# Alternating heads in the chunk products of a recurrence, with an accumulator bank for each head

## The chip, the cores and the metric

One core of a Trainium2 chip runs the whole computation as one program. The metric is the device time of the program in microseconds; the time before is the median of three runs. The engines are TensorE (PE, with its weight loads shown as PEld), VectorE (DVE), ScalarE (ACT), GpSimd (POOL) and SyncE (SP), which issues most DMAs.

## The reference, cut to what matters

Two transformer-like blocks run one after the other on a sequence of 1024 tokens of width 1024, in float32. The first has attention and a state space model side by side, then a gated feed-forward. The second has a retention mixer (4 heads of 128) and an RWKV-7 mixer (8 heads of 64) side by side, then a feed-forward and a gated embedding. The change lies in the RWKV-7 mixer, a recurrence over time with a 64 by 64 state for each head:

```
def step(state, inp):
    r_t, w_t, k_t, v_t, kk_t, b_t = inp
    sa = einsum('bhvk,bhk->bhv', state, -kk_t)
    state = state * w_t[:, :, None, :] + sa[..., None] * b_t[:, :, None, :] + v_t[..., None] * k_t[:, :, None, :]
    return state, einsum('bhvk,bhk->bhv', state, r_t)
```

The kernel computes it by chunks of 64 steps. Within a chunk, the products of all pairs of steps (s, t) of the keys (k and b = kk * a, each divided by the running decay) with the queries (-kk and r, each times the running decay) are one matrix product per head, masked to s < t or s <= t.

## The kernel before, in words

The program has stages in a row: the first block, its feed-forward, then `phase_mixers` (the retention and the recurrence of the second block, about 1365 to 1990 us of the profile), then its output projection, feed-forward and final gate. A planner orders the instructions of each engine when the program is built: an instruction's priority is its place in the order of issue, moved ahead by the number given to `high_priority`, and the planner takes, at each point of its own timeline, the ready instruction of highest priority. At run time each engine works through its order.

In `phase_mixers` generators are merged step by step, in proportion to weights; each `yield` ends a step. The recurrence has 16 quarters (4 pairs of heads by 4 quarters of the sequence; a quarter has 4 chunks of 64 for each of two heads). At step i four generators of it run beside each other: `rw_chain` of quarter i-2 (moved ahead by 300), `rw_tail` of i-3 (not moved ahead), `rw_solve` of i-1 (100) and `rw_pre` of i (200). With them run the retention (`ret_all`) and the projections (`rw_proj`), not moved ahead, whose products of three float32r matmuls each (`mm3`, line 149) are most of TensorE's work.

`rw_pre` holds the change. It builds AR (queries, two heads in partitions 0 to 63 and 64 to 127) and KB (keys, likewise; its halves are written by VectorE at line 1498 and GpSimd at line 1507, one head after the other). Then, head by head, four products of KB and AR (line 1514), one per chunk, each over 64 partitions, go into one accumulator bank of the tag "r0", and VectorE masks the bank into AA[:, h] (line 1517). The trace prints the tag as r. Parts of AA go to memory by eight small DMAs (line 1523) and come back re-ordered as As (line 1525), on which `rw_solve` begins with fifteen rounds on VectorE (line 1563). The rest of `rw_pre` transposes KB (line 1531) and prepares VU and the bonus.

The tag "r0" has two banks. `rw_pre` uses them for five further results (lines 1474, 1529, 1536, 1543), `rw_solve` for its products (line 1592, 1597 and 1604, written with the chunks in the outer loop and the heads in the inner), and `rw_tail` for its transposes (line 1692), which VectorE reads at line 1697. A product of float32 shows in the trace as two weight loads and two matmul records.

Of the kernel before, what the change touches and what calls it, by code (L numbers as in the profile page):

```python
# [13 lines left out]
ALU = mybir.AluOpType  # L14
# [52 lines left out]
class Builder:  # L67
# [1368 lines left out]
    def rw_pre(self, n, p, ps, B, D):  # L1436
# [5 lines left out]
        V, G, AC, TE = nc.vector, nc.gpsimd, nc.scalar, nc.tensor  # L1442
# [11 lines left out]
        def tmp(tag, bufs=1):  # L1454
            return self.t(p, [128, 256], tag=tag, bufs=bufs)
# [4 lines left out]
        a, s = tmp("a", 2), tmp("s", 2)  # L1460
# [23 lines left out]
        AR = D["AR"] = self.t(p, [128, 4, 2, 64], tag="AR", bufs=3)  # L1484
# [8 lines left out]
        KB = self.t(p, [128, 4, 2, 64], tag="KB", bufs=2)  # L1493
        V.scalar_tensor_tensor(d, k, kkw, a, ALU.mult, ALU.mult)
        yield
        for h in range(2):
            q = slice(64 * h, 64 * h + 64)
# [7 lines left out]
        for h in range(2):  # L1505
            q = slice(64 * h, 64 * h + 64)
            G.tensor_tensor(KB[q, :, h], ch(u)[q], ch(Pi)[q], ALU.mult)
            yield
        AA = D["AA"] = self.t(p, [128, 2, 4, 2, 64], tag="AA", bufs=3)
        for h in range(2):  # L1510
            q = slice(64 * h, 64 * h + 64)
            pa = self.t(ps, [128, 4, 2, 64], tag="r0", bufs=2)
            for c in range(4):
                TE.matmul(pa[:, c].rearrange("p m t -> p (m t)"), KB[q, c].rearrange("p m s -> p (m s)"),  # L1514
                          AR[q, c].rearrange("p m t -> p (m t)"), start=True, stop=True)
            yield
            V.tensor_tensor(AA[:, h], pa, B["mask"].unsqueeze(1).to_broadcast([128, 4, 2, 64]), ALU.mult)
            yield
        ds = self.t(self.dram, [4, 2, 4, 16, 16], tag="ds", bufs=2)
        for h in range(2):  # L1520
            for b in range(4):
                o = 64 * (1 - h) + 16 * b
                self.store("d").dma_start(ds[:, 1 - h, b].rearrange("c j i -> j c i"), AA[o : o + 16, h, :, 0, 16 * b : 16 * b + 16])
        A = D["A"] = self.t(p, [128, 256], tag="As", bufs=ASB)
# [19 lines left out]
        for c in range(4):  # L1544
            for h in range(2):
                q = slice(64 * h, 64 * h + 64)
                TE.matmul(pv[q, c], ch(v)[q, c], self.C["fold"][q], start=True, stop=True)
        yield
        for h in range(2):
            q = slice(64 * h, 64 * h + 64)  # L1550
# [3 lines left out]
    def rw_solve(self, n, p, ps, B, D):  # L1554
# [26 lines left out]
        def per(f):  # L1581
            px = self.t(ps, [128, 4, 64], tag="r0", bufs=2)
            for c in range(4):
                for h in range(2):
                    f(px[H[h], c], h, c)
            return px
# [9 lines left out]
        yield  # L1596
        px = per(lambda o, h, c: TE.matmul(o, D["AA"][H[h], 1 - h, c, 0], Mt[H[h], c], start=True, stop=True))
        yield
# [12 lines left out]
    def rw_chain(self, n, p, ps, B, D):  # L1611
# [4 lines left out]
        H = [slice(0, 64), slice(64, 128)]  # L1616
        AR, AA, KBt, TT, VU, pc = (D[x] for x in ("AR", "AA", "KBt", "TT", "VU", "pc"))
        if qt == 0:
            self.rwS = None
        py = self.t(ps, [128, 4, 64], tag="ry", bufs=1)  # L1620
        for c in range(4):
            S = self.rwS
            px = self.t(ps, [128, 64], tag="rc", bufs=1)
            for h in range(2):
                TE.matmul(px[H[1 - h]], AA[H[h], h, c, 0], VU[H[h], c, h], start=True, stop=S is None)
                if S is not None:
# [27 lines left out]
            for h in range(2):  # L1654
                TE.matmul(py[H[h], c], AA[:, h, c, 1], VU[:, c, h], start=True, stop=S is None)
                if S is not None:
# [570 lines left out]
```

## Time and profile before

| | |
|---|---|
| median of 3 runs | 2825.08 us (2824.87 to 2826.22) |
| the profiled execution's own time | 2825.83 us |
| its span, first to last instruction | 2824.1 us |
| TensorE busy | 2739.6 us, 97% of the span |
| VectorE busy | 1762.4 us, 62% |
| ScalarE, GpSimd busy | 1138.1 us (40%), 631.0 us (22%) |
| mean granted TensorE clock | 0.982 of full speed |

Busy time is the time in which an engine had an instruction under way; records of TensorE overlap, so a row of x16 lasts from the first start to the last end. The chain that ended last is followed back from the last instruction of the program; an engine's share of it says how much of the time that engine's work was what the end waited for. In the timeline, neighbouring instructions of one engine and one line are merged, with their count behind the x; the rows of weight loads are left out here.

### The profile page before, as it was taken

To read this page: it belongs to the slowest core of one execution; us is meant where nothing else is said; L and a number is where in the kernel's file an instruction comes from. 1 tells how busy PE (TensorE), PEld (TensorE's weight loads), DVE (VectorE), ACT (ScalarE), POOL (GpSimd) and SP (SyncE) were. 2 spreads that over 40 slices of the span, in tenths; PEclk is the share of its full clock that TensorE was granted. 3 is DMA by queue.
4 is the path that set the end of the run, shared out by engine and by line. 5 is a ranking of instruction groups with operands and counts; after the bars stand their busy time and mean duration, and the time that the engine had idled before them with its cause. 6 is when DMAs were issued, how large, how long until landed. Compare 5 with 4: busy or idle time off the path is not lost.

```text
span 2824.1 us, 44346 instructions
## 1 busy us (share of the span) xinstructions
PE 2739.6 (97%) x16624; PEld 2282.3 (81%) x16624; DVE 1762.4 (62%) x3481; ACT 1138.1 (40%) x2210; POOL 631.0 (22%) x1096
## 2 busy tenths in 40 slices
PE   7998998999999999999999999999999999999998
PEld 6987987877878888887888788887787878888887
DVE  6654667378666665463656675775558666665463
ACT  4233566444333344455333333334434333344352
POOL 5024533143111110030132231424131111110010
PEclk9999998999999999999999999999999999999999
DMA  4111020243545566565211211213714545576532
GB/s 144 47 42 55 14 86 15 90 149 101 175 161 186 178 226 211 190 208 183 63 55 41 57 54 41 57 46 103 254 53 141 173 166 180 179 278 204 171 127 86
DMA packets 173808, 352.10 MB, mean 125 GB/s; under 512 B 37785, under 2 KB 83065, under 8 KB 173593
## 3 DMA queue, kind: packets, MB, share of 16 engines
q1 hardware_dynamic: 152248, 277.43, 30.0%
q0 software_dynamic: 21344, 71.84, 7.2%
q8 instruction: 130, 2.13, 0.3%
q14 instruction: 86, 0.70, 0.1%
HBM read 246.90 MB, written 102.30 MB: 124 GB/s over the span
## 4 chain that ended last, share of the span: by engine, by line
PE 73%; issue 11%; DVE 6%; DMA 4%; POOL 3%; ACT 3%; SPq 0%; POOLq 0%; DVEq 0%; ACTq 0%
PE y L149 19%; PE mm L149 16%; PE x L149 7%; PE o L149 6%; PE z L149 6%; PE tr L149 3%; PE r L1514 1%; PE r L1604 1%; PE tr L200 1%; PE ry L1657 1%; POOL rp L641 1%; PE u L149 1%; PE o L758 1%; DVE w L104 1%; DMA td<-w_dn 1%
## 5 line engine op out<-in xcount | busy, mean ns | idle before, releaser
L103 ACT ACTIVATE w<-raw 128x1024 fp32r<-128x1024 f32 (+1 forms) x324 | 286.3, 889 | 407.5 <-PE y L149 140.2
L104 DVE TENSOR_TENSOR w<-raw,w 128x1024 fp32r<-128x1024 f32 (+1 forms) x324 | 330.4, 1024 | 121.7 <-ACT w L103 109.4
L149 PE MATMUL y<-h,w 128*128 128x512 f32 x1152 | 286.8, 390 | 4.8 <-DVE v L353 3.3
L149 PE MATMUL y<-w,h 128*128 128x512 f32 x1152 | 267.3, 391 | 0.0
L149 PE MATMUL mm<-w,h 128*128 128x256 f32 (+1 forms) x1632 | 260.3, 300 | 2.1 <-ACT w L103 2.1
L149 PEld LDWEIGHTS y<-h,w 128*128 128x128 f32 x1152 | 215.5, 188 | 51.5 <-DVE v L353 4.9
L149 PEld LDWEIGHTS y<-w,h 128*128 128x128 f32 x1152 | 215.1, 188 | 44.5 <-ACT mix L1260 0.3
L149 PEld LDWEIGHTS mm<-w,h 128*128 128x128 f32 x1632 | 221.3, 191 | 22.1 <-ACT w L103 2.9
L149 PE MATMUL y<-hx,w 128*128 128x512 f32 x960 | 233.8, 391 | 1.2 <-ACT hx L103 0.9
L149 PEld LDWEIGHTS y<-hx,w 128*128 128x128 f32 x960 | 180.5, 189 | 40.9 <-ACT hx L103 1.8
L104 DVE TENSOR_TENSOR h<-dr,h 128x512 fp32r<-128x512 f32 x154 | 102.5, 687 | 136.2 <-ACT h L103 131.1
L149 PE MATMUL mm<-h,w 128*128 128x512 f32 x672 | 183.1, 408 | 4.1 <-DVE lx L1377 2.6
L149 PE MATMUL o<-w,h 128*128 128x512 f32 x768 | 182.1, 393 | 2.8 <-DVE mix L1270 1.6
L149 PE MATMUL x<-h,w 128*128 128x512 f32 x672 | 175.3, 392 | 0.0
L149 PEld LDWEIGHTS o<-w,h 128*128 128x128 f32 x768 | 142.4, 188 | 33.3 <-DVE mix L1270 2.2
L103 ACT ACTIVATE h<-dr 128x512 fp32r<-128x512 f32 x154 | 92.8, 624 | 176.4 <-DMA dr<-ff 82.3
L149 PE MATMUL mm<-w,xh 128*128 128x256 f32 x768 | 155.2, 297 | 4.6 <-ACT qk L631 3.4
L376 DVE TENSOR_TENSOR t<-raw,raw 128x512 f32<-128x512 f32 x40 | 29.5, 738 | 189.2 <-DMA raw<-w_ffn 189.2
L149 PEld LDWEIGHTS x<-h,w 128*128 128x128 f32 x672 | 124.8, 188 | 26.2 <-ACT w L103 0.9
L149 PEld LDWEIGHTS mm<-h,w 128*128 128x128 f32 x672 | 120.1, 190 | 31.9 <-DVE lx L1377 2.8
L149 PE MATMUL z<-h,w 128*128 128x512 f32 x576 | 143.6, 396 | 1.9 <-ACT s L367 1.1
L251 POOL DMA_DIRECT2D ff<-v x66 | 36.4, 552 | 474.7 <-DVE v L361 467.1
(527 smaller groups left out, 5503.4 us busy)
## 6 DMA issues: line engine op xcount, KB each, us to landing
raw<-w_ffn SPq DMA_DIRECT2D x88, 512.0 KB
dr<-ff SPq DMA_DIRECT2D x70, 512.0 KB
ff<-v POOLq DMA_DIRECT2D x88, 256.0 KB, 3.1
td<-w_dn SPq DMA_DIRECT2D x44, 512.0 KB
td<-td POOLq DMA_DIRECT2D x44, 512.0 KB, 3.7
raw<-td SPq DMA_DIRECT2D x40, 512.0 KB
ff<-sd POOLq DMA_DIRECT2D x66, 256.0 KB, 4.9
raw<-w_dn SPq DMA_DIRECT2D x30, 512.0 KB
```

The lines of the kernel that those rows point to most:

```text
L103: self.nc.scalar.activation(hi, src, AF.Copy)
L104: self.nc.vector.tensor_tensor(lo, src, hi, ALU.subtract)
L149: return self.nc.tensor.matmul(*a, **kw, skip_group_check=more)
L200: nc.tensor.transpose(p[:, 128 * j : 128 * j + 128], xs[j][:, 128 * k : 128 * k + 128], self.ident)
L251: self.store("v").dma_start(self.part(("ff", {(0, 0): 0, (1, 0): 1, (1, 1): 2}[m, n]), f // 2), v)
L376: V.tensor_tensor(t[:, lo], r[1][:, lo], r[0][:, lo], ALU.subtract)
L641: nc.gpsimd.tensor_tensor(o, a, b, ALU.mult)
L758: nc.tensor.matmul(po, l, r, start=l is am, stop=False)
L1514: TE.matmul(pa[:, c].rearrange("p m t -> p (m t)"), KB[q, c].rearrange("p m s -> p (m s)"), AR[q, c].rearrange("p m t -> p (m t)"), start= ...
L1604: px = per(lambda o, h, c: TE.matmul(o, E[H[h], c], W[H[h], c], start=True, stop=True))
L1657: TE.matmul(py[H[h], c], AR[H[h], c, 1], S[H[h]], start=False, stop=True)
```

## The change

The two accumulators are taken first, one for each head. The eight products of a quarter are issued in one step, chunks in the outer loop and heads in the inner one. The two masked copies follow, each in a step of its own. `rw_pre` has three yields here where it had four.

```diff
         AA = D["AA"] = self.t(p, [128, 2, 4, 2, 64], tag="AA", bufs=3)
+        pa = [self.t(ps, [128, 4, 2, 64], tag="r0", bufs=2) for _ in range(2)]
+        for c in range(4):
+            for h in range(2):
+                q = slice(64 * h, 64 * h + 64)
+                TE.matmul(pa[h][:, c].rearrange("p m t -> p (m t)"), KB[q, c].rearrange("p m s -> p (m s)"),
+                          AR[q, c].rearrange("p m t -> p (m t)"), start=True, stop=True)
+        yield
         for h in range(2):
-            q = slice(64 * h, 64 * h + 64)
-            pa = self.t(ps, [128, 4, 2, 64], tag="r0", bufs=2)
-            for c in range(4):
-                TE.matmul(pa[:, c].rearrange("p m t -> p (m t)"), KB[q, c].rearrange("p m s -> p (m s)"),
-                          AR[q, c].rearrange("p m t -> p (m t)"), start=True, stop=True)
-            yield
-            V.tensor_tensor(AA[:, h], pa, B["mask"].unsqueeze(1).to_broadcast([128, 4, 2, 64]), ALU.mult)
+            V.tensor_tensor(AA[:, h], pa[h], B["mask"].unsqueeze(1).to_broadcast([128, 4, 2, 64]), ALU.mult)
             yield
```

## Rows read from the trace of the kernel before

**Rows 1.** The page: busy time of two engines, and the chain that ended last.
```profile
PE 2739.6 (97%) x16624; PEld 2282.3 (81%) x16624; DVE 1762.4 (62%) x3481; ACT 1138.1 (40%) x2210; POOL 631.0 (22%) x1096
...
PE 73%; issue 11%; DVE 6%; DMA 4%; POOL 3%; ACT 3%; SPq 0%; POOLq 0%; DVEq 0%; ACTq 0%
```

**Rows 2.** Stretches: length, busy PE, PEld, DVE, ACT, POOL, clock, DMA share, GB/s.
```profile
1365.00:1910.00 545.00, 541.26 (x5298) 455.08 (x5296) 370.83 (x1161) 196.90 (x559) 161.59 (x309) 1.00 0.18 52
```

**Rows 3.** Line 1514 (ns min/median/max); the chain by line, 1365 to 1990 us.
```profile
L1514 PE MATMUL r<-AR,KB x256: 272/272/400, 1370.1 to 1908.7; 64*128 64x128 f32 x128
...
by line: PE mm L149 48.7%; PE r L1514 4.7%; PE r L1604 4.4%; PE ry L1657 4.0%; PE ry L1655 3.5%; PE rc L1645 1.8%; issue 1.8%; PE rc L1634 1.7%; PE rc L1625 1.7%; PE r L1597 1.6%; PE r L1692 1.5%; PE r L1475 1.3%; DMA As<-ds 1.3%; PE rt L17
```

**Rows 4.** Order on TensorE, heads together (start us, us, engine, line, count).
```profile
1370.15 1.71 PE L1514 MATMUL r<-AR,KB 64*128 64x128 f32 x16
...
1907.27 1.71 PE L1514 MATMUL r<-AR,KB 64*128 64x128 f32 x16
1908.91 0.34 PE L1625 MATMUL rc<-VU,AA 64*64 64x64 f32 x4
```

**Rows 5.** Order on TensorE where the tail is near, one quarter of the middle.
```profile
1807.64 0.44 PE L1692 MATMUL r<-c_fold,yc 64*64 64x64 f32 x6
...
1809.79 1.16 PE L1514 MATMUL r<-AR,KB 64*128 64x128 f32 x8
1810.88 1.09 PE L149 MATMUL mm<-w,h 128*128 128x256 f32 x7
...
1813.79 1.16 PE L1514 MATMUL r<-AR,KB 64*128 64x128 f32 x8
1814.87 0.27 PE L1692 MATMUL r<-c_fold,yc 64*64 64x64 f32 x1
```

**Rows 6.** The same, the first and the last such quarter.
```profile
1476.41 0.32 PE L1692 MATMUL r<-c_fold,yc 64*64 64x64 f32 x2
1476.67 1.16 PE L1514 MATMUL r<-AR,KB 64*128 64x128 f32 x8
...
1480.89 1.16 PE L1514 MATMUL r<-AR,KB 64*128 64x128 f32 x8
...
1879.50 1.16 PE L1514 MATMUL r<-AR,KB 64*128 64x128 f32 x8
```

**Rows 7.** Order on TensorE, in the two split quarters without a tail.
```profile
1389.57 1.26 PE L1514 MATMUL r<-AR,KB 64*128 64x128 f32 x12
...
1393.83 0.48 PE L1514 MATMUL r<-AR,KB 64*128 64x128 f32 x2
...
1778.00 0.71 PE L1514 MATMUL r<-AR,KB 64*128 64x128 f32 x4
1778.64 0.33 PE L1634 MATMUL rc<-X,TT 64*64 64x64 f32 x4
1778.90 0.71 PE L1514 MATMUL r<-AR,KB 64*128 64x128 f32 x4
1779.54 0.62 PE L149 MATMUL mm<-w,h 128*128 128x256 f32 x3
```

**Rows 8.** Waits of TensorE, then VectorE: us in total, times, longest.
```profile
PE ry L1655 <- ACT VU L1636: 1.7, 3, 0.9
PE rc L1634 <- DVE TT L1607: 1.3, 2, 0.9
...
DVE Tm L1563 <- POOL As L1526: 21.6, 14, 3.9
```

**Rows 9.** A loop over chunks outside and heads inside, in the solve.
```profile
1445.44 0.68 PE L1592 MATMUL r<-c_ident,M 64*64 64x64 f32 x16
```

**Rows 10.** Order on VectorE: KB, masked copies, and the tail's read of its bank.
```profile
1815.59 0.48 DVE L1697 SCALAR_TENSOR_TENSOR ysq<-r,c_rwc,bv 128x256 f32<-128x256 f32 x1
...
1905.95 1.28 DVE L1498 TENSOR_TENSOR KB<-d,Pi 64x256 f32<-64x256 f32 x2
...
1908.46 1.29 DVE L1517 TENSOR_TENSOR AA<-r,c_rwmask 128x512 f32<-128x512 f32 x2
```

## The prediction

> **What bounds the kernel now.** I read the busy shares and the chain of waits first, then the stretches, then the order of instructions on TensorE around line 1514. TensorE is busy 97% of the span, and the chain that ended last lies 73% on it [rows 1]. The edited lines run only in the recurrence, and there TensorE is the bound: 541.26 of 545.00 us busy at a granted clock of 1.00 (the 2.4 GHz level), VectorE 370.83 [rows 2]. TensorE's longest waits there come to 1.7 and 1.3 us in total, before the chain's products and not before line 1514 [rows 8]. So in this stretch a microsecond taken off TensorE's queue should come off the span, less whatever wait appears behind it. The 256 records of line 1514 carry 4.7% of the chain between 1365 and 1990 us, 29 us [rows 3].
>
> **What one quarter costs now.** Each of the 16 quarters has 8 products (2 heads by 4 chunks), and each product shows as two records, so 16 a quarter. One head alone is "x8", 1.16 us from first start to last end; the next work starts 1.09 us after it (1809.79 to 1810.88) [rows 5]. One record lasts 0.272 us [rows 3], so the eight starts spread over 0.89 us, about 0.11 us apart. Three patterns occur.
> Seven quarters have both heads back to back: x16, 1.71 us, next work after 1.64 us; the first and the last are shown [rows 4]. That is less than twice 1.09, because records of the second head already run beside the last ones of the first: 16 starts fit in 1.71 - 0.27 = 1.44 us, where two heads in a row would take twice 0.89.
> Nine quarters have the heads apart, which costs twice 1.09 = 2.17 us. In seven of these (one in the middle, the first and the last are shown) the tail's products of line 1692 are around them, so the tail holds one of the two "r0" banks [rows 5, 6]. In the other two no tail is near: other products stand between the heads and inside the second one, which is x2 and x2 behind an x12 in one, and x4 and x4 in the other [rows 7].
>
> **The change part by part.** Nothing is computed that was not computed before: 8 products and 2 masked copies a quarter stay.
> *The order of the products.* Heads use different halves of the partitions. The trace has a loop of just this form, chunks outside and heads inside: line 1592 with 16 records in 0.68 us, each about 0.22 us long, so 16 starts in 0.46 us [rows 9]. The blocks of one head show records 0.11 us apart for 128 columns; with 64 columns and two heads at once, 0.46 us for 16 is two records per 0.06 us. Two streams there run side by side at full pace. So I take an alternated block as long as one head alone: 16 starts in 0.89 us, next work after 1.09 us.
> Seven quarters: 7 x (1.64 - 1.09) = 3.85 us. The two split ones without a tail: the eight products are now issued in one step of the generator, with nothing of the other generators between them: 2 x (2.17 - 1.09) = 2.2 us.
> The Trainium skill ("TensorE: Matmul & The Clock Gate", Part 3, "The mechanism") says that matmuls start and end strictly in program order. By that a head's second record would hold back the other head's first, one more step of 0.11 us per quarter, and the sum below would be 1.2 us smaller. The 0.46 us of line 1592 has no room for the extra step; the row decides.
> *Both accumulators at once.* Now the first two products need both r0 banks. In the seven quarters with a tail, the second bank is free only once line 1697 has read the tail's result. The planner puts whatever is ready first, so head 0's four products can still go alone and head 1's after that read: the old order, nothing won. Upper bound, if the tail moves out of the way each time: 7 x 1.08 = 7.6 us. Lower bound, below nothing: head 1 has started up to 2.2 us before line 1697 began, recycling the bank of head 0 (1813.79 against 1815.59 plus 0.48 [rows 5, 10], so 2.3 us to the end of the read); if TensorE simply stood for that in all seven, it loses 7 x 2.3 = 16 us. I take two of seven quarters won, 2.2 us: in six of the other quarters that have a tail it is already finished before line 1514, so small shifts of phase decide, while the nearest rows all show the bank held.
> *The masked copies.* Two on VectorE, 1.29 us in a row [rows 10]. They already come back to back behind a contiguous block; the chunk matrix then would be complete at 1907.27 + 1.16 + 1.29 = 1909.7, where it is now (1908.46 + 1.29). So nothing is won or lost for the DMA behind it. In the two splits without a tail it is complete up to 4 us sooner (the second head's records begin at 1393.83 in the one, 4.3 us behind the first's [rows 7]); the wait behind it (VectorE at line 1563 for the reloaded matrix, 21.6 us over 14 times [rows 8]) is hidden by TensorE's other work, and I count nothing.
> *One step fewer in the generator.* From four yields to three, so everything behind it in each quarter is offered slightly earlier and the planner orders the recurrence anew. Cost unknown in sign. The nearest rows are split blocks: a head cut in two takes 0.64 + 0.64 us to the next work, 0.2 us more than 1.09 [rows 7]. The small products of the chain, the solve and the tail are cut like that all over the stretch; twenty cuts more or fewer are plus or minus 4 us. I take zero and keep this for the range.
>
> **The sum.** 3.85 + 2.2 + 2.2 = 8.2 us off TensorE's queue. TensorE's idle time is under 1% there; I let 0.9 us be given back to new waits: 7.3 us. The profiled execution took 2825.83 us (span 2824.1), so 2818.5; the median of before lies 0.75 us lower, so about 2818 us.
>
> **The rivals.**
> 1. *The heads stay apart where a tail is near, and part of the rest is lost.* Only 3.85 + 2.2 = 6.0 us, or less where head 1's half of KB comes behind head 0's (the two writes of line 1498 take 1.28 us one after the other [rows 10]). With a few cuts more: 1 to 5 us off, 2822 us. For it: all seven tail rows. Against it: a later phase could free them. The Trainium skill ("TensorEngine Tiling (Array Packing)", "PSUM Bottleneck") says that tiling speeds TensorE but not the emptying of the accumulators, which can become the limit. By it the 3.85 us would not come, since the two masked copies end where they end now: 8.2 - 3.85 = 4.4 us, less what is given back, 2822 too. The trace agrees on when the copies end [rows 4, 10], but TensorE, not the copies, has no idle time [rows 2], so I hold it for the less likely.
> 2. *Every quarter alternates in full.* 3.85 + 2.2 + 7.6 = 13.6 us: 2812 us. For it: in six quarters the tail is done in time already. Against it: the tail is issued at the lowest priority, and its bank stays taken from its first product to the end of line 1697's read, 8.4 us in the quarter of the middle (1807.64 to 1816.07 [rows 5, 10]).
> 3. *The bank ring starves, slower.* Place: TensorE at head 1's first product, waiting for line 1697. With all products of a quarter in one step at high priority, the plan has them in front of work that would have filled the wait; behind the waiting product stand all the chain's and the retention's products, since TensorE issues in order. Price up to 16 us, against 6.0 us won in the other nine: 2835 us at worst, and 2832 us with 1.9 us of standing in each (13 - 6.0). It decides from 0.9 us of standing per tail quarter on (6.0 / 7). For it: the second head now always asks for the bank that the tail holds. Against it: the planner does not place a product whose bank it believes taken, so only its misjudgement counts.
>
> **How the numbers follow.** My forecast 0.33, rival 1 0.30, rival 2 0.20, rival 3 0.17. Within 0.2% (5.65 us, about what can be told from no change) lies rival 1; faster are the forecast and rival 2, 0.53; slower is rival 3, 0.17. The range from 2809 to 2831 leaves out the far ends of rivals 2 and 3. The forecast's own range is 2814 to 2820.
>
> **What would show it.** Line 1514 as x16 in about 1.16 us per quarter, and its share of the chain falling from 29 to 18 us, shows the alternation; x8 in 1.16 us next to line 1692 shows rival 1. A wait of TensorE on VectorE's line 1697, at line 1514, shows rival 3. If line 1514 falls as forecast and the stretch does not shorten, the new plan gave the time back, and the pieces of the other small products will be more. Wrong outright: 16 records that still take 1.7 us, so that heads do not run side by side at 128 columns.

## The result, and the profile after

The changed kernel takes 2846.82 us (median of 4 runs, 2843.67 to 2850.41), the kernel before 2824.97 on the same chip (4 runs, 2823.23 to 2826.22): a ratio of 1.0072 [1.0059, 1.0085] (in brackets, here and below, the 95% interval). The forecast was 2818, its range ended at 2831: wrong in its sign. Measured a second time (run e5_after_again below) the ratio was 1.0050 [1.0035, 1.0064], so the loss is 14 to 20 us by the two medians.

The profiled execution took 2845.48 us, 19.7 more than that of before. The instructions ahead of the first edited product have the same order in both kernels, yet that product starts 4.4 us later (1374.57 against 1370.15 [rows 4]); in other executions of the same code it lay up to 3.5 us earlier than in the kernel before (1366.66 in m2 below), so this part is spread between executions. From there to the first product of the next stage (2046.14, before 2027.79) it is 671.6 us against 657.6: 14 us. Behind it 1.3 us are left. The 14 us are what has to be explained; this piece is called the stretch below. In the profiled execution of e5, the same program, it is 667.2 us, 9.6 us longer than before, so its length in one execution is known to some 4 us.

The page of the kernel after (busy time; the chain that ended last by engine) answers [rows 1]:

```profile
PE 2743.3 (96%) x16624; PEld 2284.2 (80%) x16624; DVE 1761.7 (62%) x3481; ACT 1136.6 (40%) x2210; POOL 631.8 (22%) x1096
...
PE 68%; issue 11%; DVE 8%; DMA 7%; POOL 3%; ACT 3%; SPq 0%; POOLq 0%; DVEq 0%; ACTq 0%
```

TensorE lost five points of the chain, to VectorE and to DMAs above all. The windows of the kernel after say where (columns as in [rows 2]; the recurrence, then the end of the stage in two parts):

```profile
1369.40:1949.40 580.00, 573.22 (x5702) 481.89 (x5700) 388.49 (x1228) 209.21 (x602) 179.30 (x340) 0.99 0.18 51
1949.40:1989.40 40.00, 31.39 (x299) 23.41 (x298) 19.63 (x52) 15.59 (x47) 12.57 (x24) 0.87 0.40 136
1989.40:2046.10 56.70, 43.19 (x190) 32.18 (x189) 31.59 (x52) 23.04 (x39) 4.41 (x11) 0.91 0.71 242
```

The same in the kernel before:

```profile
1365.00:1945.00 580.00, 576.09 (x5714) 485.63 (x5712) 390.95 (x1230) 210.68 (x606) 180.18 (x344) 1.00 0.18 51
1945.00:1985.00 40.00, 36.40 (x310) 26.30 (x309) 21.38 (x59) 16.38 (x47) 11.54 (x24) 0.91 0.49 167
1985.00:2027.80 42.80, 38.41 (x168) 30.06 (x168) 28.55 (x44) 21.93 (x36) 3.32 (x8) 0.92 0.83 283
```

At the end of the stage TensorE is busy for 74.6 us in both (31.39 + 43.19; 36.40 + 38.41 = 74.8), but in 96.7 us where it was 82.8. All of the loss is TensorE standing: 22.1 us against 8.0. Over the whole stretch TensorE is busy 642.7 us, where it was 645.7, and idle 28.9, where it was 11.9: 3 us less work and 17 us more standing, 14 of them at the end and 2.9 in the 580 us ahead of it (6.8 us idle, where it was 3.9). Its waits between 1920 and 2045 us, kernel after (total us, times, longest; w is weights of the output projection after ScalarE's part of their preparation, S the recurrence's state, X an intermediate result of it, ryy the retention's tile):

```profile
PE mm L149 <- ACT w L103: 7.5, 3, 5.9
PE rc L1626 <- DVE S L1652: 4.9, 1, 4.9
PE rt L1787 <- POOL ryy L1784: 2.6, 1, 2.6
PE rc L1635 <- ACT X L1631: 2.5, 2, 2.1
```

And in the kernel before, where the product of line 1625 (1626 after) does not stand for S here at all:

```profile
PE mm L149 <- ACT w L103: 2.1, 2, 1.1
PE mm L149 <- ACT rkv L103: 1.7, 2, 1.1
...
PE rt L1786 <- POOL ryy L1783: 1.0, 3, 0.6
```

(Behind line 1516 the kernel after has every line one number higher.) The first two waits of after are taken below as two separate losses. Neither is at the edited products. In e5 the four waits of after are 7.1, 3.9, 2.6 and 2.6 us.

**The edited products.** Line 1514 by lines, kernel after (busy us, mean ns, idle ahead of it; in the kernel before the same view has 33.2 us):

```profile
L1514 PE MATMUL r<-AR,KB 64*128 64x128 f32 x256 | 31.3, 288 | 0.0
```

And the order on TensorE:

```profile
1374.57 1.16 PE L1514 MATMUL r<-AR,KB 64*128 64x128 f32 x16
1375.66 1.20 PE L149 MATMUL mm<-h,w 128*128 128x512 f32 x4
...
1553.08 1.16 PE L1514 MATMUL r<-AR,KB 64*128 64x128 f32 x8
...
1557.44 1.16 PE L1514 MATMUL r<-AR,KB 64*128 64x128 f32 x8
...
1815.36 1.71 PE L1514 MATMUL r<-AR,KB 64*128 64x128 f32 x16
```

The quarter at 1374.57 alternates: x16 in 1.16 us, next work 1.09 us after the start. Two more do (x16 at 1441.78 in 1.16 and at 1664.16 in 1.17 us), two in part, and one is cut behind x14 without alternating (e1 below, which has no alternation, shows the same x14). In eight quarters the heads still come apart, as at 1553.08, and in two they come one behind the other, as at 1815.36 in 1.71 us [rows 4]. TensorE saved 1.9 us of busy time at this line (33.2 - 31.3), not 8.2.

**Loss one, the state step.** Before the projection begins, SyncE issues the reloads of its input, and ScalarE (line 103) and VectorE (line 104) split each tile into two parts. SyncE's order in the kernel after (start us, us, queue, line, transfer, count):

```profile
1954.38 7.07 SPq L1791 DMA_DIRECT2D cT<-ro  x2
1962.75 3.48 SPq L1841 DMA_DIRECT2D rkv<-cT  x5
```

In the kernel before:

```profile
1951.91 0.32 SPq L1790 DMA_DIRECT2D cT<-ro  x1
1953.49 2.22 SPq L1840 DMA_DIRECT2D rkv<-cT  x5
```

The first of the five reads the retention tile that the store ahead of it has just written; it goes 1.6 us behind that store in both. Counted from the first edited product it goes 4.8 us later than before (1962.75 - 1374.57 = 588.2 us against 1953.49 - 1370.15 = 583.3). What ScalarE does meanwhile, kernel after (the bracket is the idle time ahead of a row and what ended it):

```profile
1962.68 0.20 ACT L1638 COPY VU<-rc 64x64 f32<-64x64 f32 x1
1966.02 0.63 ACT L103 ACTIVATE h<-rkv 128x512 fp32r<-128x512 f32 x1 [3.13 <-DMA rkv<-cT]
1967.94 0.63 ACT L103 ACTIVATE h<-rkv 128x512 fp32r<-128x512 f32 x1 [1.29 <-DMA rkv<-cT]
1968.92 0.63 ACT L103 ACTIVATE h<-rkv 128x512 fp32r<-128x512 f32 x1 [0.35 <-DMA rkv<-cT]
1970.79 0.63 ACT L103 ACTIVATE h<-rkv 128x512 fp32r<-128x512 f32 x1 [1.24 <-DMA rkv<-cT]
1971.33 0.33 ACT L1643 ACTIVATE Sd<-S,pc 128x64 f32<-128x64 f32 x1
```

VectorE beside it:

```profile
1966.68 0.69 DVE L104 TENSOR_TENSOR h<-rkv,h 128x512 fp32r<-128x512 f32 x1 [2.75 <-ACT h L103]
1967.29 0.29 DVE L1776 BATCH_NORM_STATS2 rbs<-rt 128x6 f32<-128x128 f32 x1
1968.60 0.69 DVE L104 TENSOR_TENSOR h<-rkv,h 128x512 fp32r<-128x512 f32 x1 [1.02 <-ACT h L103]
1969.21 0.28 DVE L1652 SCALAR_TENSOR_TENSOR S<-rc,pc,Sd 128x64 f32<-128x64 f32 x1
```

And TensorE behind VectorE's state step:

```profile
1964.34 0.33 PE L1658 MATMUL ry<-S,AR 64*64 64x64 f32 x2
1969.54 0.48 PE L1626 MATMUL rc<-VU,AA 64*64 64x64 f32 x4 [4.87 <-DVE S L1652]
```

The reader is to see a queue in order: four splits stand in a row on ScalarE, and their data come late. Behind them on ScalarE stands Sd, the decayed state of the recurrence; on VectorE the second halves of the first two splits, which wait for ScalarE, stand ahead of the retention's own statistics (line 1776) and of S, the new state. In the kernel before the same splits have this work between them:

```profile
1956.38 0.63 ACT L103 ACTIVATE h<-rkv 128x512 fp32r<-128x512 f32 x1
1957.54 0.63 ACT L103 ACTIVATE h<-rkv 128x512 fp32r<-128x512 f32 x1 [0.54 <-DMA rkv<-cT]
1958.08 0.33 ACT L1642 ACTIVATE Sd<-S,pc 128x64 f32<-128x64 f32 x1
1958.31 0.61 ACT L103 ACTIVATE h<-rkv 128x512 fp32r<-128x512 f32 x1
```

**Loss two, the weights.** Later, ScalarE in the kernel after has the splits of the feed-forward's first weights (raw) ahead of those of the projection's weights (rkv), for which TensorE stands until 2006.12 (5.91 us):

```profile
2003.21 1.06 ACT L103 ACTIVATE w<-raw 128x1024 fp32r<-128x1024 f32 x1 [2.56 <-DMA raw<-w_ffn]
2004.48 1.06 ACT L103 ACTIVATE w<-raw 128x1024 fp32r<-128x1024 f32 x1 [0.21 <-DMA raw<-w_ffn]
2005.45 2.17 ACT L103 ACTIVATE w<-rkv 128x512 fp32r<-128x512 f32 x4
```

In the kernel before four splits of the projection's weights come first:

```profile
1988.10 0.62 ACT L103 ACTIVATE w<-rkv 128x512 fp32r<-128x512 f32 x1
1991.27 1.67 ACT L103 ACTIVATE w<-rkv 128x512 fp32r<-128x512 f32 x3 [2.54 <-DMA cT<-ro]
1994.22 1.06 ACT L103 ACTIVATE w<-raw 128x1024 fp32r<-128x1024 f32 x1 [1.29 <-DMA raw<-w_ffn]
```

### The profile page after: what moved, and what is told of

Same layout as the page of the kernel before. It is cut to its first block, busy times and chain, and to the rows that moved or that the text cites. A ratio compares the mean times of both kernels' runs of the same rounds, so it can differ in the third digit from the quotient of the medians.

```text
span 2843.7 us, 44325 instructions
## 1 busy us (share of the span) xinstructions
PE 2743.3 (96%) x16624; PEld 2284.2 (80%) x16624; DVE 1761.7 (62%) x3481; ACT 1136.6 (40%) x2210; POOL 631.8 (22%) x1096
## 4 chain that ended last, share of the span: by engine, by line
PE 68%; issue 11%; DVE 8%; DMA 7%; POOL 3%; ACT 3%; SPq 0%; POOLq 0%; DVEq 0%; ACTq 0%
PE y L149 18%; PE mm L149 15%; PE x L149 7%; PE o L149 6%; PE z L149 5%; PE tr L149 3%; DMA raw<-w_ffn 2%; DVE w L104 2%; PE tr L200 1%; PE r L1514 1%; PE r L1605 1%; PE ry L1658 1%; POOL rp L641 1%; PE u L149 1%; PE o L758 1%
```

## The experiments

Every kernel ran against the kernel before on the same chip. Times and ratios are over all runs; the other columns are from the one profiled execution of each. "Tile" is when ScalarE makes the last retention tile, counted from the first edited product; "S" and "w" are TensorE's total waits at the end of the stage for VectorE's state step and for ScalarE's w of line 103.

| run | ratio | stretch | tile | S | w |
|---|---|---|---|---|---|
| before | 1 | 657.6 | 617.7 | 0 | 2.1 |
| after | 1.0072 [1.0059, 1.0085] | 671.6 | 625.7 | 4.9 | 7.5 |
| e5_after_again | 1.0050 [1.0035, 1.0064] | 667.2 | 622.2 | 3.9 | 7.1 |
| e1_onestep | 1.0054 [1.0039, 1.0068] | 672.3 | 628.0 | 0 | 5.9 |
| e2_hold | 1.0028 [1.0016, 1.0041] | 663.9 | 624.4 | 4.6 | 2.1 |
| e3_three | 1.0017 [1.0008, 1.0027] | 659.1 | 618.3 | 0 | 2.1 |
| e4_tail_rt | 1.0112 [1.0098, 1.0127] | 689.5 | 627.2 | 5.5 | 0.4 |
| e6_before_hold | 1.0001 [0.9991, 1.0011] | 659.4 | 618.9 | 0 | 1.9 |
| e7_4yields | 1.0021 [1.0006, 1.0037] | 660.8 | 620.5 | 0 | 1.7 |
| e8_4yields_hold | 1.0031 [1.0018, 1.0044] | 668.3 | 628.1 | 0 | 3.4 |
| i_after_act | 1.0042 [1.0029, 1.0054] | 668.3 | 625.0 | 2.5 | 5.8 |
| i_after_act_hold | 1.0022 [1.0012, 1.0032] | 666.3 | 623.3 | 2.9 | 3.8 |
| i_before_act | 1.0018 [1.0009, 1.0028] | 662.5 | 617.4 | 0 | 7.3 |
| i_before_act_hold | 1.0001 [0.9992, 1.0010] | 657.7 | 616.9 | 0 | 2.5 |
| m1_after_k3last | 1.0011 [1.0002, 1.0021] | 657.2 | 619.0 | 0 | 1.0 |
| m2_after_behind4 | 1.0023 [1.0014, 1.0033] | 659.9 | 618.7 | 0.2 | 1.7 |
| m3_before_behind4 | 1.0016 [1.0007, 1.0024] | 659.7 | 617.4 | 4.0 | 2.7 |
| m4_before_k3last | 1.0028 [1.0017, 1.0039] | 663.0 | 622.5 | 4.1 | 2.6 |
| n1_after_k3last_only | 1.0033 [1.0024, 1.0043] | 666.7 | 621.7 | 0 | 7.0 |
| n2_before_tail_rt | 1.0087 [1.0073, 1.0102] | 677.4 | 615.8 | 0.4 | 0 |

### Which part of the change: e1, e3, e7, e8, e5

e1 keeps the one step and both banks but issues head 0 before head 1; e3 alternates in three quarters only, which have three yields each, and leaves the steps of the others as before; e7 gives the changed kernel its fourth yield back; e8 is e7 with the edit of e2 (below); e5 is the changed kernel again.

```diff
e1:  -        for c in range(4):
     -            for h in range(2):
     +        for h in range(2):
     +            for c in range(4):
e3:  +        if n in (0, 6, 8):   (the changed form)
     +        else:                (the form before, one head per step)
e7:       for h in range(2):
              V.tensor_tensor(AA[:, h], pa[h], ...)
              yield
     +    yield
```

Expected of e1: 

> Both accumulator banks are taken first and the eight products come in one step, as in the change, but head by head (heads in the outer loop). The order of the engines is then nearly that of the changed kernel; only the alternation is gone. Theory A (the alternation itself gains a little, the new order of the stage loses the time): 2848 us (2844 to 2852), 1 to 3 us above the changed kernel. Theory B (alternating heads or their two banks are what costs): back near before, 2825 to 2830 us.

Expected of e3: 

> Heads alternate in three of the sixteen quarters (0, 6 and 8), where they were back to back before; the other quarters as before. The order of all engines stays that of the kernel before except near these quarters. Theory A: line 1514 as x16 in 1.16 us there, 3 x 0.55 = 1.6 us faster, 2823.4 us (2821 to 2825.5). Theory B: three sixteenths of the loss, 4 us slower, 2829 us.

Expected of e5: 

> The changed kernel itself once more, beside the next three. The first 1360 us, before the first edited instruction, are the same program in all kernels, and took 1359 to 1367 us in the profiles so far, so part of the 20 us may lie there. Theory A: 2840 to 2847 us; the stretch from the first edited product to the first product of the next stage 13 to 15 us longer than before (657.7 us there), in every profile.

Expected of e7: 

> The changed kernel with a fourth yield behind the masked copies, so that the recurrence's preparation has as many steps as before. Heads alternate as in the changed kernel (both banks first, eight products in one step), the whole stage is ordered anew once more, but in this order the last two retention tiles, not three, come behind the recurrence's last products, and the feed-forward's loads stand as before. Theory A: the end's loss is gone, 2824 to 2830 us, with the stretch from first edited product to next stage 655 to 660 us. Theory B (alternation or its banks cost): as the changed kernel, 2840 to 2847 us.

Expected of e8: 

> The kernel of e7_4yields with the feed-forward's first loads held back as in e2_hold. Theory A: as e7_4yields within 3 us, since there these loads do not delay the projection; 2824 to 2830 us.

e1 has no alternation and loses as much as the changed kernel: the loss belongs to the new steps (both banks first, eight products in one step, three yields), not to the order of the products. Its last tile is as late as after's and its w wait is 5.9 us. It has loss one too, at another instruction: three splits stand on ScalarE ahead of a copy of the recurrence's VU, and TensorE stands for that copy instead of for S. The rows are from ScalarE and, the last, from TensorE:

```profile
1961.96 0.63 ACT L103 ACTIVATE h<-rkv 128x512 fp32r<-128x512 f32 x1 [2.45 <-DMA rkv<-cT]
1964.00 1.32 ACT L103 ACTIVATE h<-rkv 128x512 fp32r<-128x512 f32 x2 [1.41 <-DMA rkv<-cT]
1965.34 0.21 ACT L1637 COPY VU<-rc 64x64 f32<-64x64 f32 x1
...
1965.60 0.48 PE L1656 MATMUL ry<-VU,AA 128*64 128x64 f32 x2 [5.02 <-ACT VU L1637]
```

With the fourth yield back (e7) the end is as in the kernel before: 50.1 us from the last product of line 1636 (1634 in the kernel before) to the next stage, where before has 49.8 and after 64.5. But alternation is nearly gone from the order too (line 1514 takes 34.2 us), and the kernel is still 2 to 10 us slower. e8, with both edits, is no better: its recurrence took 618.0 us to that product (before 607.9), in an order that was not taken apart further. So four yields do not by themselves restore the time; which part of the new steps makes the bad order was not separated. e3 went against its theory A: line 1514 took 1.2 us less than before (32.0 us), as meant, but TensorE's idle time in the recurrence grew by 1.4 us, and the kernel is slower by 1.0017. That is the size of theory B, three sixteenths of the loss; its stretch is 1.5 us longer than before, less than one execution can tell, so where those 4 to 5 us lie is open. e5 fell short of the band expected, in time (2838.8 us) and in the stretch (9.6 us longer, not 13 to 15).

### The weights: e2 and its control e6

Both put the first loads of the feed-forward's weights behind the last load of the projection's weights for its first half.

```diff
-                nc.sync.dma_start(raw, self.I["w_o"][...])
+                ld = nc.sync.dma_start(raw, self.I["w_o"][...])
+                if th == 0:
+                    self.hold = ld
```

Expected of e2: 

> The changed kernel, with the first weight loads of the second feed-forward ordered behind the last w_o load of the first half of the output projection. The order of the recurrence stays that of the changed kernel; only a few places at the end of the stage move. Theory A has two parts in the last 40 us of the stage: the retention's last tile comes 8 to 12 us later, and the feed-forward's loads and their splits stand in front of the projection's. If the second part is real: 4 to 8 us below the changed kernel, 2839 to 2843 us. If the late tiles are all of it: 2847 us as the changed kernel. Theory B: 2847 us too.

Expected of e6: 

> The kernel before, with the first weight loads of the second feed-forward ordered behind the last w_o load of the first half, as in e2_hold. In the kernel before these loads stand in front of part of the projection's loads too, but after the last retention tile, and they were 40.0 us from that tile to the next stage's first product. Theory A: nothing to win there, 2826 us within 3. If these loads cost something in any order: 4 to 6 us faster.

The w wait falls from 7.5 to 2.1 and the ratio to 1.0028; in the kernel before, where the wait is 2.1 anyway, the edit does nothing. Against e5, the changed kernel of the same chip, that is 0.0022 or 6 us, though the two intervals overlap a little; the pair n1 and m1 below differs by as much (1.0033 and 1.0011), and there the intervals lie apart. So loss two is shown, at about 6 us. The S wait stays at 4.6 and the tile stays late.

### A theory that fell: i_after_act and its three companions

I first took SyncE for the cause: two retention stores in front of the five reloads [SyncE's row at 1954.38 above].

```diff
-        self.store("r").dma_start(self.S["cT"][h, :, tk], o)
+        (nc.scalar if h == 3 and t >= 4 else self.store("r")).dma_start(self.S["cT"][h, :, tk], o)
```

Expected of i_after_act: 

> The kernel after, with one edit: the retention's stores of the last head's last four tiles are issued from ScalarE's queue, right behind the activation that makes the tile, and not from SyncE's. The order on TensorE, VectorE and GpSimd is that of the kernel after, instruction by instruction. Theory A (SyncE stands at a retention store whose tile isn't done, five reloads of the projection's input stand behind it, and VectorE and ScalarE stand at the splits of these, ahead of the recurrence's state step and of the retention's own work): the last retention tile comes 7 to 9 us sooner (about 618 us behind the first edited product, not 622 to 626), and the kernel is about 8 us faster than the kernel after, 2829 to 2837 us, ratio to the kernel before 1.001 to 1.004. Rival (the retention's tile is late because its products come late in TensorE's order; the store only shows it): the last tile stays at 622 to 626 us, ratio 1.005 to 1.007.

Expected of i_after_act_hold: 

> The same, and the first loads of the feed-forward's weights are put behind the output projection's own loads. Theory A (two causes, about 8 us by the retention stores on SyncE and about 6 us by these weight loads): both losses gone, the stretch from the first edited product to the next stage 655 to 659 us as in the kernel before (657.7), ratio 0.997 to 1.001. If alternation's gain on line 1514 (2.1 us) reaches the end, it lies in the lower half of that. Rival (the loss is spread over the recurrence's new order): ratio 1.003 or more, as with the weight loads alone held back (1.0028).

Expected of i_before_act: 

> The kernel before with the stores alone moved to ScalarE's queue. Theory A: in its order only one store stands ahead of the reloads, and it goes out without standing, so nothing to win: ratio 0.999 to 1.001, last retention tile at 616 to 619 us. Rival (ScalarE's queue is a better place for these stores whatever the order): faster by 3 us or more, ratio under 0.999.

Expected of i_before_act_hold: 

> The kernel before with both edits. Theory A: neither loss is there, so 0.999 to 1.001 as with the weight loads held back alone (1.0001). Rival: as in the line before, ratio under 0.999. Compared with the kernel after with both edits it says what the alternation itself is worth once the end of the stage is repaired: 0 to 3 us.

The tile stayed at 625.0 and 623.3: theory A missed, though the ratios, 1.0042 and 1.0022, lie between its bands and the rival's. The edit could not help, since the four stores that it moves come behind the reloads; the two in front are of tiles 2 and 3, and the first of the five reloads reads tile 3, so it has to come after them on any queue. That is in the kernel before too; there only the tile is earlier. i_before_act missed on the other side: slower, 1.0018. Its profile shows a w wait of 7.3 us, which the order after this edit brought without any alternation, and with the weight loads held back it is gone (1.0001). That is loss two a second time, by itself.

### The splits in front of the state step: m1 to m4, n1

m1 and m4 put the reload that waits for the late tile last of the eight, in the changed kernel and in the kernel before; m2 and m3 put the five reloads behind the store of the next retention tile; these four have the edit of e2 as well. n1 is m1 without it.

```diff
m1, m4, n1:
-                    self.o_load(0, ct[0], range(8), pk, "rkv", RKV),
+                    self.o_load(0, ct[0], (0, 1, 2, 4, 5, 6, 7, 3), pk, "rkv", RKV),
m2, m3, in ret_tile and in o_load:
+        if h == 3 and t == 4:
+            self.late = ins
...
+            if th == 0 and k >= 3:
+                self.after(ins, self.late)
```

Expected of m1: 

> The kernel after, the feed-forward's first weight loads held back, and the projection's reload of the late retention head's tile put last of the eight, so that the four others don't stand behind it. The splits of those four come well ahead in ScalarE's and VectorE's order and their data are there. Theory C (the engines stand at splits whose data wait for the late retention tile, with the recurrence's state step behind them): the wait of TensorE's product of line 1626 on the state step (4.87 us in the kernel after) goes, the last retention tile comes at 615 to 619 us behind the first edited product, not 622 to 626, and the ratio is 0.997 to 1.001. Rival D (the new order of the recurrence itself has the retention's tiles late, the splits only stand where time is left over): tile at 621 or later, ratio 1.002 to 1.004.

Expected of m2: 

> The kernel after, the weight loads held back, and the five reloads put behind the store of the next retention tile, so two state steps of the recurrence go ahead of the first split. Theory C: the last retention tile 5 to 9 us sooner than in the kernel after (615 to 619), the projection starts later by about as much as the reloads do (up to 8 us) and takes part of it back: ratio 0.998 to 1.002. Rival D: tile at 621 or later, ratio 1.003 or more.

Expected of m3: 

> The kernel before (no alternation), the weight loads held back, and the five reloads put behind the store of the next retention tile: ScalarE's order then has all five splits in a row ahead of a state step of the recurrence, as the kernel after has it. Theory C: the loss appears without the alternation, 5 to 9 us, last retention tile at 622 to 627, ratio 1.002 to 1.003. Rival D: 616 to 620 as in the kernel before, ratio 0.999 to 1.001.

Expected of m4: 

> The kernel before with the reload of the late tile put last and the weight loads held back: control for m1. In the kernel before ScalarE's splits of these tiles already have state steps between them, so theory C gives at most 2 us: ratio 0.999 to 1.000. Its difference to m1 is what the alternation is worth in an order that doesn't stand at the splits: theory C 0 to 3 us in favour of m1, rival D 4 us or more against it.

Expected of n1: 

> The kernel after with the reload of the late retention head's tile put last, and nothing else. If the two causes add up, the weight loads' share stays: m1 (1.0011) plus what holding them back gave the kernel after (1.005 to 1.007, less 1.0028): ratio 1.003 to 1.005. The wait of line 1626 on the state step is gone and the last retention tile comes at 617 to 621. If the late tile was the cause of both, it is 1.0011 as with both edits.

In m1 the wait for S is gone, the tile is at 619.0 and the stretch at 657.2 us, that of the kernel before; the ratio, 1.0011, lies just above theory C's band. TensorE's waits at the end of the stage in m1:

```profile
PE rt L1787 <- POOL ryy L1784: 2.6, 1, 2.6
...
PE mm L149 <- ACT w L103: 1.0, 1, 1.0
```

In m3, which has no alternation, five splits stand in a row on ScalarE ahead of Sd, three on VectorE ahead of S, and TensorE stands there as in the kernel after:

```profile
1962.98 0.34 PE L1625 MATMUL rc<-VU,AA 64*64 64x64 f32 x4 [4.04 <-DVE S L1651]
```

With e1 that is a third kernel in which TensorE stands behind these splits, and two of the three have no alternation. So the stand comes from that order of splits, whatever made it. In m1 rival D fails (the tile is sooner by 5 us). In m3 neither is right throughout: the stand is there, as theory C says, but its price was put too high, 2.0 to 6.8 us and not 5 to 9, and the last tile comes at 617.4, as D says, since the retention makes the delay up (586 and 602 us for the tiles on either side of the stand). m2 all but removes the wait for S too (0.2 us, tile at 618.7), but its ratio, 1.0023, lies just above theory C's band; the projection starts later, as foreseen: 62.6 us from the last product of line 1635 to the next stage. m4 missed: its new order runs into the wait for S by itself (4.1 us), so it is no clean control, and the difference between m1 and m4 says nothing of the alternation.

n1 has loss two alone, and the two add up within the intervals (1.0050 for e5, 1.0028 without loss two, 1.0033 without loss one, 1.0011 without both), and TensorE's wait is the one of the weights:

```profile
PE mm L149 <- ACT w L103: 7.0, 1, 7.0
```

### More alternation: e4 and its control n2

The tail's product gets a bank of the retention's tag, so that "r0" is free for both heads.

```diff
-        po = self.t(ps, [128, 4, 64], tag=PO, bufs=2 if PO == "r0" else 1)
+        po = self.t(ps, [128, 512], tag="rt", bufs=2)[:, 0:256].rearrange("p (c t) -> p c t", c=4)
```

Expected of e4: 

> The changed kernel, with the tail's products (line 1692 of before) in a bank of the retention's tag rt instead of r0, so the second bank is free more often. The stage is ordered anew. Theory A: heads alternate in about nine quarters instead of three to five, TensorE's time at line 1514 falls from 29 us to 21 to 24 us; the total then depends on when the retention's last tile ends, 2820 to 2845 us. Theory B: more alternation, slower than the changed kernel, over 2850 us.

Expected of n2: 

> The kernel before with the tail's product in a bank of the retention's tag: control for the kernel after with the same edit (1.0112, recurrence 638 us, TensorE idle 26.8 us). If the retention's two banks are the cause, the loss is here too: ratio 1.006 or more, recurrence over 620 us. If the loss came from the alternation that the free bank allowed, the ratio is 0.998 to 1.003 and the recurrence 605 to 612 us.

The view by lines of e4 for the edited products:

```profile
L1514 PE MATMUL r<-AR,KB 64*128 64x128 f32 x256 | 25.4, 299 | 0.0
```

7.8 us less than before (33.2): with the bank free seven quarters alternate in one block and two more in two pieces, and nearly all of the forecast's 8.2 us at this line is there. But the kernel takes 2858.1 us, as theory B said, and the recurrence to its last product of line 1635 took 638.1 us, 30 more than before, with 26.8 us idle (6.5 before). n2 has the bank moved without alternation and loses 1.0087 and 19 us there: most of e4's loss is the bank taken from the retention, as expected of the first case. The idle time is not all of it: in both the granted clock of the recurrence was lower (0.94 in e4 and 0.95 in n2, 0.99 before), and TensorE was busy longer (611.5 and 609.8 us, 601.6 before). So what full alternation is worth with no other tag made poorer was not measured.

## Why the prediction was wrong

*What bounds the kernel.* TensorE bounds the recurrence, and that held: 573.22 of 580.00 us busy. It was used further than the rows carried. In the kernel after TensorE had 3 us less work in the stretch and stood 2.9 us longer ahead of the stage's end; in e3 1.2 us saved at line 1514 came back as 1.4 us idle; and m1, with 1.9 us saved there and both losses gone, is still 0.6 to 5.9 us slower than before. That "a microsecond taken off TensorE's queue should come off the span" was not seen at this size in any run; where those few us go is open, since single executions differ by more.

*The cost of an alternated quarter* was right to the digit: x16 in 1.16 us, next work 1.09 us after the start, as line 1592 had suggested [rows 9], without an extra step of 0.11 us.

*How many quarters alternate* was wrong: 11 were counted (7 contiguous, 2 split, 2 of the tail's), 3 do in full and 2 in part. Rival 1 was nearer: heads stay apart beside the tail in five of its seven quarters, and in the other two come one behind the other without alternating. Of the seven quarters that were contiguous, which both counted as won, three alternate in full and the last two have come apart; whether the bank or head 1's half of KB decides there was not tested. This step missed by 6.3 us (1.9 saved for 8.2). Two readings on the way were off without weight in the sum: in the first split quarter the second head's records begin inside the x12, at 1390.1, and only its last four at 1393.83; and head 1 started 1.8 us before line 1697 began in the rows shown, not 2.2 (the 2.3 us to the end of the read are right).

*"One step fewer in the generator ... I take zero"* is the step that failed, with its bound of plus or minus 4 us. e1, which has the new steps and no alternation, is slower by 1.0054. What it left out is the planner's new order as a whole and not the count of yields alone: e7, which has the fourth yield back, ends the stage as before, but e8 with four yields has a stretch of 668.3 us. Its size was 14 us in the stretch, 9.6 us in e5's. The bound came from cuts of small products on TensorE [rows 7], the wrong place to look: in the 575 us behind the first edited product the blocks into which all products but the mm3 ones are cut number 1160, against 1177 before, so there were no more cuts. Instead the new order moved other queues, some 575 us behind the first edited product, where the retention, the recurrence and the projection's first loads meet. There two groups of splits came to stand in front of work that TensorE needs: 4.9 us for S and 2.1 more for X behind it (2.5, and 0.4 before), 5.4 us more for w (7.5 against 2.1), 1.6 more for the retention's tile (line 1787). Together 14.0 us, where TensorE stands 14.1 us longer (22.1 - 8.0); among the smaller waits one of 1.7 us went and several of 0.3 to 0.6 came.

*Rival 3* had the right sign by luck, for another reason: no wait for line 1697's read (1698 after) at line 1514 appears in the trace, and the view by lines has 0.0 us idle ahead of that line. *The masked copies* cost nothing that shows, as said; the only wait of TensorE for them in the recurrence is 0.3 us, at line 1532.

*What would show it* named the right suspect: "If line 1514 falls as forecast and the stretch does not shorten, the new plan gave the time back". Its condition was not met, as line 1514 fell by 1.9 us only, and the time went into whole waits, not into more pieces of small products.

No run beat the kernel before. m1 repairs both losses and comes to 1.0011.

## What to carry to other kernels

When a planner orders the queues, an edit that changes the number of steps is an edit of everything behind it; price it by the places where a queue in order holds work that waits for a transfer in front of work that the bound engine needs, such as the seam to the next stage, and not by the engine edited. Read such a seam on ScalarE's, VectorE's and SyncE's timelines of the kernel before, and ask which row would stand if one tile came 5 us later. And run the step change without the purpose of the edit: e1 alone would have told the sign.

## What the runs showed of the hardware

**The clock falls in both kernels at the seam**, and not only behind the stand. In the kernel after TensorE stood from 1964.5 to 1969.5, then (columns as above, the granted clock ahead of the DMA share):

```profile
1964.50:1969.50 5.00, 0.17 (x2) 0.03 (x1) 1.80 (x5) 1.84 (x3) 0.35 (x1) 0.92 0.81 249
1969.50:1979.00 9.50, 7.32 (x41) 4.88 (x41) 4.82 (x9) 4.31 (x12) 1.97 (x3) 0.50 0.37 125
```

In the kernel before it was busy for 9.82 of 11 us, and the clock went to the lower of its two levels (1.2 of 2.4 GHz) all the same:

```profile
1945.00:1956.00 11.00, 9.82 (x138) 7.70 (x137) 6.09 (x20) 3.66 (x14) 4.52 (x11) 1.00 0.63 232
1956.00:1963.00 7.00, 6.71 (x52) 5.45 (x52) 5.29 (x13) 5.43 (x15) 1.90 (x4) 0.52 0.66 212
```

So both kernels have a clock at its lower level here, and TensorE's busy time to the end of the stage is the same (74.6 and 74.8 us): the clock is not what sets them apart. Why it fell in the second case the trace does not say.

**Identical code spreads by 8 us between executions.** Up to the first edited product, where the kernels have the same code, the profiled executions took from 1358.5 us (e8) to 1366.7 us (after), counted from the first product. A kernel's total, one execution against one, cannot tell 4 us here. Nor can the stretch behind a common point: for the changed kernel it was 671.6 us in one execution and 667.2 in the other (e5). The largest waits in it repeat better: 4.9 and 3.9 us for S, 7.5 and 7.1 for w.
